# Operand rows at one position modulo 256 bytes, and short f16 products ahead of runs of weight products

## The chip, the core and the metric

The kernel runs on one core of a Trainium2 chip. The metric is the device time of one execution in microseconds; the median of several executions is compared.

## What is computed

The reference runs 256 tokens of width 1024 through two blocks, in float32. The first has two layers, each a mixer and a product-key expert layer (peer); the second has a feed-forward, a token mixer over 16 meta tokens and the 256 tokens, and another feed-forward.

```python
for layer in range(2):
    xn = rmsnorm(h, norm_mix[layer])
    h = h + (attn_retention_mixer if layer == 0 else short_conv_mixer)(xn, ...)
    h = h + peer(rmsnorm(h, norm_ffn[layer]), ...)
x = rmsnorm(h, final_norm)
...
h = h + 0.5 * swiglu(rms_norm(h, ffn1_norm), ffn1_w_in, ffn1_w_out)
h = h + token_mixer(rms_norm(h, mix_norm), ...)
h = h + 0.5 * swiglu(rms_norm(h, ffn2_norm), ffn2_w_in, ffn2_w_out)

def peer(xn, w_q, sub_keys, u, v):       # 8 heads x 2 key halves, 128 x 128 experts
    q = xn @ w_q                         # scores against the sub keys, top 16 of each half,
    gate = softmax(top 16 of the sums)   # top 16 of the 256 pairs
    return sum over chosen experts k of gate[k] * gelu(xn . u[k]) * v[k]
```

## The kernel before

**Tiling.** Activations lie transposed: 128 features on the partitions, tokens along the row, so that `h` is 8 chunks of 272 columns (16 meta tokens, then 256 tokens). Every expert is computed for every token in peer, and a gate matrix that is zero for those not chosen multiplies the result.

**Weight products.** Each weight tile is 128x1024 f32, 512 KB. `Weights` loads tiles on SP's queue three ahead (`wraw`), and splits each into a rounded part `whi` (ACT, line 177) and a rest `wlo` (DVE, line 178), three tiles ahead of their use. Activations are split in the same way (`split`, line 308). `mm3` (lines 303 to 306) makes one product of three: whi with the high part, whi with the low part, wlo with the high part, all fp32r. A weight tile is eight of these, 24 matmuls of 128x128 stationary weights against a moving row of 256 (or 272) columns. The moving rows are those of `xh`/`xl`, `ph`/`pl`, `ah`/`al`, `ch`/`cl`, `zh`/`zl`, `yh`/`yl` and `oh_`/`ol_`.

**Where the rows lie.** In the built program `xh` begins 128 bytes past a multiple of 256 in each partition and its rows are 272 x 4 = 1088 bytes, 64 past a multiple. Row c therefore begins at 128 + 64c, modulo 256; the slice without the meta columns (`XC`) begins 64 bytes later. A loop over c or j passes through the positions 0, 64, 128 and 192 in turn. The same holds for the 272-column `ph` and `ah` of the first feed-forward. The 256-column `ch`, `zh`, `ph`, `yh`, `oh_` and the `ah` of the last feed-forward have rows of 1024 bytes, and small pad tiles (`cpad`, `zpad`, `ppad`, `ypad`, `apad`) place all of their rows at 192. The moving `whi` of the first mixer (512 columns) and of the token mixer's value part (324) is not touched by the change.

**Stages.** In order: mixer0; for each layer peer's query stage (16 weight tiles, `ph` as moving operand), its u stage (128 tiles, `xh`, one c after another in a tile, two tiles for each PSUM tile `ps`), its v stage (128 tiles, `xh[:, j % 8, 0:256]`, 24 products on one row j, accumulated in four `acc` tiles); mixer1 between the layers; then ffn (272 columns), the token mixer, ffn (256 columns).

**What sets the order.** Code is written in the order in which it is to run. `bg` is a list of background tasks with costs; `bg.tick` after a weight tile issues some of them. In the u stages these are the scores (f32 products, line 780), top-16 searches on DVE, transposes, and from the middle on the gate products (`mult`, lines 940 and 941: 16 f16 products of 64 columns each time). In the v stages they go on up to j = 61. Other products come between weight tiles too: column sums (line 367), spreading of the norm (line 381), the flip products (1152, 1153), and the attention of the token mixer. So weight products come in runs that other products end.

```python
    def ft_tile(ps, n, cols=None, first=True):
        hi, lo = W.get()
        for c in range(8):
            s = slice(c * 128, c * 128 + 128)
            xh_, xl_ = n.x(c, cols)
            mm3(ps, hi[:, s], lo[:, s], xh_, xl_, first and c == 0, c == 7, skip_group_check=True)
```

Of the kernel before, what the change touches and what calls it, by code (L numbers as in the profile page):

```python
# [8 lines left out]
F32 = mybir.dt.float32  # L9
F32R = mybir.dt.float32r  # L10
# [11 lines left out]
META = 16  # L22
SEQ = 256
TALL = META + SEQ
HD2 = 64
GSCALE = 16384.0
TK_Q, TK_U, TK_G, TK_V = 1.2, 1.35, 72, 60
# [218 lines left out]


def _program(tc, nc, glob, wpool, mmp, accp, drp, ins, out, scat, stop):
    V, A, P = nc.vector, nc.scalar, nc.tensor

    h = glob.tile([128, 8, TALL], F32, name="h")
    xh = glob.tile([128, 8, TALL], F32R, name="xh")
    xl = glob.tile([128, 8, TALL], F32R, name="xl")
    ident = glob.tile([128, 128], F32, name="ident")
    ones = glob.tile([128, 2], F32, name="ones")
    gains = glob.tile([128, ins["gains"].shape[1]], F32, name="gains")

    glob.tile([128, 8], F32, name="gpad")
    W = Weights(nc, wpool, 3, 3)
    for nm in ("mix0_in", "mix0_out", "wq0", "u0", "v0", "mix1_in", "mix1_out", "wq1", "u1", "v1", "ffn1_in", "ffn1_out"):  # L260
        W.add(ins[nm])
# [14 lines left out]
            nc.scalar.dma_start(scat[l][:, i * n:i * n + n], src)  # L276
            cleared[l] += 1

    nc.scalar.dma_start(gains, ins["gains"])
    V.memset(ones, 1.0)  # L280
    A.activation(ones[:, 1:2], ones[:, 0:1], AF.Square)
    nc.gpsimd.dma_start(ident, ins["ident"])
# [18 lines left out]
        return accp.tile([128, 512], F32, tag="acc", name="acc")  # L301

    def mm3(ps, wh, wl, mh, ml, start, stop, **kw):
        P.matmul(ps, wh, mh, start=start, stop=False, **kw)  # L304
        P.matmul(ps, wh, ml, start=False, stop=False, **kw)  # L305
        P.matmul(ps, wl, mh, start=False, stop=stop, **kw)  # L306

    def split(hi, lo, src):
        A.copy(hi, src)  # L309
# [81 lines left out]
    class TwoNorms(Norm):  # L391


        def __init__(self, parts, sp, newps):
            super().__init__(("ffn1_norm_2", 0), 0, parts, newps)
            self.gf = col(("final_norm", 0))
            self.s1 = sp.tile([128, TALL], F32, name="s1")
            self.bc1 = sp.tile([128, TALL], F32, name="bc1")
            a, b = gcol[("final_norm", 0)], gcol[("ffn1_norm_2", 0)]
            self.gg = sp.tile([128, 8], F32, name="gg")  # L400
            self.m2 = sp.tile([128, 3], F32, name="m2")
            V.tensor_tensor(self.gg, gains[:, a:a + 8], gains[:, b:b + 8], op=ALU.mult)
            mg = sp.tile([128, 8, META], F32, name="mg")
            V.tensor_tensor(mg, h[:, :, 0:META], gains[:, b:b + 8, None].to_broadcast([128, 8, META]), op=ALU.mult)
            split(self.hi[:, :, 0:META], self.lo[:, :, 0:META], mg)
# [40 lines left out]
            for c in range(8):  # L446
                bg.add(0.45, lambda c=c: one(c))

    def ft_tile(ps, n, cols=None, first=True):

        hi, lo = W.get()
        for c in range(8):
            s = slice(c * 128, c * 128 + 128)
            xh_, xl_ = n.x(c, cols)
            mm3(ps, hi[:, s], lo[:, s], xh_, xl_, first and c == 0, c == 7, skip_group_check=True)
# [12 lines left out]
    def out_proj(nk, kh, kl, c0, scale, norm, last=None):  # L468

        T = TALL - c0  # L470
        for m in range(8):
            ps = mmtile()
            k = 0
            while k < nk:
                hi, lo = W.get()
                for kk in range(min(8, nk - k)):
                    s = slice(kk * 128, kk * 128 + 128)
                    mm3(ps[:, :T], hi[:, s], lo[:, s], kh(k), kl(k), k == 0, k == nk - 1)
                    k += 1
# [243 lines left out]
    def peer(l, n, close_parts, open_parts):  # L723
# [158 lines left out]
        def normed(c):  # L882
            t = glob.tile([128, TALL], F32, tag="nt", name="nxn", bufs=2)
            V.scalar_tensor_tensor(t[:, META:], h[:, c, META:], n.g(c), n.bc[:, META:], op0=ALU.mult, op1=ALU.mult)
            W.later(lambda: split(xh[:, c, META:], xl[:, c, META:], t[:, META:]))

        for q in range(16):
            if q % 2 == 0:
# [29 lines left out]
        def gates(half, newps, cost):  # L918
# [17 lines left out]
            def mult(q):  # L936
                a, bh, bl = st.pop(q)
                ps = newps()
                for t in range(8):
                    P.matmul(ps[:, t * 64:t * 64 + 64], a[:, t], bh[:, t], start=True, stop=False)  # L940
                    P.matmul(ps[:, t * 64:t * 64 + 64], a[:, t], bl[:, t], start=False, stop=True)
                st[("p", q)] = ps

            def fold(q):
# [51 lines left out]
        for jp in range(64):  # L996
# [59 lines left out]
    def ffn(c0, n, nxt, last=None, after=None):  # L1056
        T = TALL - c0
        cols = slice(c0, TALL)
        with tc.tile_pool(name=f"ffn{c0}", bufs=1) as sp:
            sp.tile([128, 48], F32, name="apad")  # L1060
            ah = sp.tile([128, 22, T], F32R, name="ah")
            al = sp.tile([128, 22, T], F32R, name="al")
            for i in range(22):
                pg, pu = mmtile(), mmtile()
                g0 = sp.tile([128, T], F32, name="fg0", bufs=2)
# [12 lines left out]
                        split(ah[:, i], al[:, i], u0)  # L1078
                    W.later(rest)

                ft_tile(pg[:, :T], n, cols)
                if i == 0:
                    n.sums()
                else:
# [5 lines left out]
                            after()  # L1090
                    gate()
                bg.tick(0.6)
                ft_tile(pu[:, :T], n, cols)
                if i == 0:
                    n.more()
                    first = gate, up
# [67 lines left out]
    def tokmix(n, BT, mknext):  # L1164
        with tc.tile_pool(name="tok", bufs=1) as sp:
# [235 lines left out]
            def kq_tiles(b):  # L1401
                t0, t1 = BATCH[b]
                for i in range(t0, t1):
                    ps = mmtile()
                    ft_tile(ps[:, (0 if is_key(i) else META):TALL], n, slice(0 if is_key(i) else META, TALL))
# [39 lines left out]

            for i in range(16):
                ps = mmtile()
                ft_tile(ps[:, :256], n, XC)
                tick()
                if i > 11 and busy():  # L1450
                    a_step()
# [14 lines left out]
            for m in range(8):  # L1466
                pf, pw = mmtile(), mmtile()
                hi, lo = W.get()
                if m < 7:
                    sigm(m + 1)  # L1470
                for k in range(8):
# [12 lines left out]

    pools = []

    def open_parts(make, T=SEQ):
# [4 lines left out]
        hi = sp.tile([128, 8, T], F32R, name="ph")  # L1492
        lo = sp.tile([128, 8, T], F32R, name="pl")
        sp.tile([128, 72], F32, name="ppad")
        return make((hi, lo), sp)

# [80 lines left out]
```

## Time and profile before

| | |
|---|---|
| median of 3 runs | 2455.16 us (2449.33 to 2455.28) |
| the profiled execution | 2454.97 us |
| its span, first to last instruction | 2453.2 us |
| TensorE matmul busy | 2427.3 us, 99%, 20410 records |
| VectorE busy | 1841.1 us, 75% |
| ScalarE busy | 1208.5 us, 49% |
| GpSimd busy | 643.0 us, 26% |
| mean rate of the DMAs | 189 GB/s |

Matmuls are pipelined: each record lasts longer than the distance to the next start, so their durations add up to more than the span. The distance between starts is read from a timeline, or as a stretch divided by the records in it. A window counts every record that touches it, so two products or so that began before its edge are in its count.

### The profile page before, as it was taken

To read this page: it belongs to the slowest core of one execution; us is meant where nothing else is said; L and a number is where in the kernel's file an instruction comes from. 1 tells how busy PE (TensorE), PEld (TensorE's weight loads), DVE (VectorE), ACT (ScalarE), POOL (GpSimd) and SP (SyncE) were. 2 spreads that over 40 slices of the span, in tenths; PEclk is the share of its full clock that TensorE was granted. 3 is DMA by queue.
4 is the path that set the end of the run, shared out by engine and by line. 5 is a ranking of instruction groups with operands and counts; after the bars stand their busy time and mean duration, and the time that the engine had idled before them with its cause. 6 is when DMAs were issued, how large, how long until landed. Compare 5 with 4: busy or idle time off the path is not lost.

```text
span 2453.2 us, 50327 instructions
## 1 busy us (share of the span) xinstructions
PE 2427.3 (99%) x20410; PEld 2363.4 (96%) x20410; DVE 1841.1 (75%) x3514; ACT 1208.5 (49%) x1745; POOL 643.0 (26%) x421
## 2 busy tenths in 40 slices
PE   8999999999999999999999999999999999999999
PEld 6799999999999999999999999999999999779999
DVE  6688896877986667788977869976677655667764
ACT  4555555444444445555554444444455443446543
POOL 0007787802320000037877403310010000100000
PEclk9999999999999999999999999999999999999999
DMA  7578887765666665667777656666655555325555
GB/s 241 171 247 218 224 225 191 173 189 192 196 206 204 215 204 186 196 177 174 180 184 178 181 175 204 202 203 212 210 191 182 173 174 172 114 95 174 188 185 168
DMA packets 170650, 464.37 MB, mean 189 GB/s; under 512 B 52369, under 2 KB 54425, under 8 KB 169905
## 3 DMA queue, kind: packets, MB, share of 16 engines
q1 hardware_dynamic: 117440, 420.04, 53.1%
q0 software_dynamic: 43616, 24.27, 7.7%
q10 hardware_dynamic: 9360, 16.84, 1.8%
q8 instruction: 160, 2.62, 0.4%
q14 instruction: 74, 0.60, 0.1%
HBM read 443.09 MB, written 17.99 MB: 188 GB/s over the span
## 4 chain that ended last, share of the span: by engine, by line
PE 91%; DVE 6%; ACT 1%; DMA 1%; issue 0%; SPq 0%; ACTq 0%; DVEq 0%
PE mm L304 18%; PE mm L306 18%; PE mm L305 18%; PE acc L304 10%; PE acc L305 10%; PE acc L306 10%; DVE wlo L178 2%; PE mm L639 1%; PE mm L640 1%; PE mm L638 1%; PE acc L1205 1%; PE acc L780 1%; ACT whi L177 0%; DVE Hb L790 0%; DVE Hb L788 0%
## 5 line engine op out<-in xcount | busy, mean ns | idle before, releaser
L178 DVE TENSOR_TENSOR wlo<-wraw,whi 128x1024 fp32r<-128x1024 f32 (+2 forms) x799 | 996.3, 1250 | 444.1 <-ACT whi L177 437.2
L177 ACT CAST whi<-wraw 128x1024 fp32r<-128x1024 f32 (+2 forms) x799 | 833.2, 1044 | 664.1 <-PE mm L305 217.1
L304 PE MATMUL mm<-xh,whi 128*128 128x256 f32 (+1 forms) x2632 | 744.0, 283 | 0.0
L306 PE MATMUL mm<-xh,wlo 128*128 128x256 f32 (+1 forms) x2632 | 741.3, 282 | 0.5
L305 PE MATMUL mm<-xl,whi 128*128 128x256 f32 (+1 forms) x2632 | 741.2, 282 | 0.0
L304 PE MATMUL acc<-xh,whi 128*128 128x256 f32 x2048 | 577.5, 282 | 0.3
L305 PE MATMUL acc<-xl,whi 128*128 128x256 f32 x2048 | 574.5, 281 | 0.2
L306 PE MATMUL acc<-xh,wlo 128*128 128x256 f32 x2048 | 574.4, 280 | 0.0
L852 POOL DMA_INDIRECT gates<-gt,idx x256 | 482.1, 1883 | 220.3 <-DVE idx L842 94.8
L304 PEld LDWEIGHTS mm<-xh,whi 128*128 128x128 f32 x2632 | 497.8, 189 | 7.8 <-issue 7.3
L306 PEld LDWEIGHTS mm<-xh,wlo 128*128 128x128 f32 x2632 | 498.3, 189 | 1.7 <-DVE wlo L178 1.7
L305 PEld LDWEIGHTS mm<-xl,whi 128*128 128x128 f32 x2632 | 495.0, 188 | 0.0
L304 PEld LDWEIGHTS acc<-xh,whi 128*128 128x128 f32 x2048 | 387.4, 189 | 0.7 <-ACT xh L309 0.7
L305 PEld LDWEIGHTS acc<-xl,whi 128*128 128x128 f32 x2048 | 386.2, 189 | 0.5 <-DVE xl L310 0.5
L306 PEld LDWEIGHTS acc<-xh,wlo 128*128 128x128 f32 x2048 | 386.5, 189 | 0.0
L306 PE MATMUL mm<-ph,wlo 128*128 128x256 f32 (+1 forms) x800 | 228.3, 285 | 5.6 <-DVE wlo L178 5.6
L304 PE MATMUL mm<-ph,whi 128*128 128x256 f32 (+1 forms) x800 | 228.9, 286 | 0.0
L305 PE MATMUL mm<-pl,whi 128*128 128x256 f32 (+1 forms) x800 | 227.3, 284 | 0.0
L306 PEld LDWEIGHTS mm<-ph,wlo 128*128 128x128 f32 x800 | 152.1, 190 | 6.4 <-DVE wlo L178 6.4
L1011 ACT ACTIVATE Hb<-mm 128x512 f32<-128x512 f32 x112 | 67.2, 600 | 180.4 <-PE mm L306 174.8
L305 PEld LDWEIGHTS mm<-pl,whi 128*128 128x128 f32 x800 | 151.4, 189 | 0.3
L304 PEld LDWEIGHTS mm<-ph,whi 128*128 128x128 f32 x800 | 151.2, 189 | 0.1
(359 smaller groups left out, 3052.9 us busy)
## 6 DMA issues: line engine op xcount, KB each, us to landing
wraw<-in_u SPq DMA_DIRECT2D x256, 512.0 KB
wraw<-in_v SPq DMA_DIRECT2D x256, 512.0 KB
wraw<-in_ffn_in SPq DMA_DIRECT2D x88, 512.0 KB
wraw<-in_mix_in SPq DMA_DIRECT2D x52, 512.0 KB
gates<-zt ACTq DMA_DIRECT2D x64, 256.0 KB
wraw<-in_wq SPq DMA_DIRECT2D x32, 512.0 KB
gj<-gates POOLq DMA_DIRECT2D x64, 256.0 KB
wraw<-in_ffn_out SPq DMA_DIRECT2D x32, 512.0 KB
```

The lines of the kernel that those rows point to most:

```text
L177: self.nc.scalar.copy(hi[:, :cols], raw[:, :cols])
L178: self.nc.vector.tensor_tensor(lo[:, :cols], raw[:, :cols], hi[:, :cols].bitcast(F32), op=ALU.subtract)
L304: P.matmul(ps, wh, mh, start=start, stop=False, **kw)
L305: P.matmul(ps, wh, ml, start=False, stop=False, **kw)
L306: P.matmul(ps, wl, mh, start=False, stop=stop, **kw)
L638: P.matmul(ps[tt], xa, hi[:, w], start=(c == 0), stop=False)
L639: P.matmul(ps[tt], xa, lo[:, w], start=False, stop=False)
L640: P.matmul(ps[tt], xb, hi[:, w], start=False, stop=(c == 7))
L780: P.matmul(t[:, i * 128:i * 128 + 128], qT[:, q, tt * 128:tt * 128 + 128], sk[:, q], start=True, stop=True)
L852: b = nc.gpsimd.indirect_dma_start(out=flat, out_offset=bass.IndirectOffsetOnAxis(ap=idx[:, i:i + 1], axis=0), in_=gt0[:, i:i + 1], in_off ...
L1011: A.activation(Haf[:, j * 256:j * 256 + 512] if j < NA else Hbf[:, (j - NA) * 256:(j - NA) * 256 + 512], ps, AF.Gelu)
L1205: P.matmul(t[:, s], KQ[pr, qt, q], KQ[pr, kt, 0:k], start=True, stop=True)
```

## The change

Rows of `xh` and `xl` become 320 floats (1280 bytes, five times 256) and a pad of 64 bytes ahead of them places every row at 192; the 256 token columns that the u stage reads stand in the last 256 floats of a row, which is 192 too. The 272-column `ph` and `ah` get rows of 320 floats of which the last 272 are used, from 192 on. `ones` moves into the tile `gains`, and `gpad` goes.

`P` becomes a wrapper that notes when a product other than a weight product or a gate product has been issued (`broken`). `settle`, called before the first product of a run's first weight tile, then issues four f16 products of 64 columns of `ident` with itself into the PSUM tile that the run is about to overwrite. It isn't called for the second tile of a `ps` in the u stage, for the single tiles of the token mixer, nor in a feed-forward while background tasks are waiting. `mult` of the gates counts as such a lead itself.

```diff
+ROW = 320
...
+    class Other:
+        broken = True
+        def matmul(self, *a, **k):
+            self.broken = True
+            return T_.matmul(*a, **k)
...
+    P = Other()
...
-    xh = glob.tile([128, 8, TALL], F32R, name="xh")
-    xl = glob.tile([128, 8, TALL], F32R, name="xl")
+    glob.tile([128, 16], F32, name="xpad")
+    xh = glob.tile([128, 8, ROW], F32R, name="xh")
+    xl = glob.tile([128, 8, ROW], F32R, name="xl")
...
+    def settle(ps):
+        if P.broken:
+            k = ident.bitcast(F16)
+            for _ in range(4):
+                T_.matmul(ps[:, 0:64], k[:, 0:128], k[:, 0:64], start=True, stop=True)
+            P.broken = False
...
-    def ft_tile(ps, n, cols=None, first=True):
+    def ft_tile(ps, n, cols=None, first=True, steady=True):
         hi, lo = W.get()
+        if first and steady:
+            settle(ps)
...
                 hi, lo = W.get()
+                if k == 0:
+                    settle(ps)
...
-                ft_tile(ps[:, s * 256:s * 256 + 256], xn, XC, s == 0)
+                ft_tile(ps[:, s * 256:s * 256 + 256], xn, slice(ROW - SEQ, ROW), s == 0)
...
-            ah = sp.tile([128, 22, T], F32R, name="ah")
+            ah = sp.tile([128, 22, row], F32R, name="ah")[:, :, row - T:]
...
-                ft_tile(pg[:, :T], n, cols)
+                ft_tile(pg[:, :T], n, cols, steady=not bg.q)
...
-    n = peer(1, made["n"], close_parts, lambda: open_parts(lambda pr, sp: TwoNorms(pr, sp, mmtile), TALL))
+    n = peer(1, made["n"], close_parts, lambda: open_parts(lambda pr, sp: TwoNorms(pr, sp, mmtile), ROW))
```

On TensorE the first u stage, behind scores that follow the second tile of a PSUM tile. Before (line 780 is the scores; 304 to 306 the weight products):

```order
L305 MATMUL mm<-xl,whi 128x256
L306 MATMUL mm<-xh,wlo 128x256
L780 MATMUL acc<-Hb 128x128 x4
L304 MATMUL mm<-xh,whi 128x256
L305 MATMUL mm<-xl,whi 128x256
```

After (line 258 is the wrapper, 329 the new products, 320 to 322 the weight products):

```order
L321 MATMUL mm<-xl,whi 128x256
L322 MATMUL mm<-xh,wlo 128x256
L258 MATMUL acc<-Hb 128x128 x4
L329 LDWEIGHTS ident
L329 MATMUL mm<-ident 128x64
L329 LDWEIGHTS ident
L329 MATMUL mm<-ident 128x64
L329 LDWEIGHTS ident
L329 MATMUL mm<-ident 128x64
L329 LDWEIGHTS ident
L329 MATMUL mm<-ident 128x64
L320 MATMUL mm<-xh,whi 128x256
```

Four f16 products stand between the scores and the weight products. There are 28 such places and 112 new products in the program.

Also on TensorE in the first u stage, behind scores that fall between the two tiles of a PSUM tile. Before:

```order
L306 MATMUL mm<-xh,wlo 128x256
L780 MATMUL acc<-Hb 128x128 x4
L304 MATMUL mm<-xh,whi 128x256
L305 MATMUL mm<-xl,whi 128x256
L306 MATMUL mm<-xh,wlo 128x256
```

After:

```order
L322 MATMUL mm<-xh,wlo 128x256
L258 MATMUL acc<-Hb 128x128 x4
L320 MATMUL mm<-xh,whi 128x256
L321 MATMUL mm<-xl,whi 128x256
L322 MATMUL mm<-xh,wlo 128x256
```

Nothing moved here; the four new products come 24 weight products later, ahead of the next PSUM tile. On DVE, ACT, POOL and SP no instruction is added, removed or moved.

## Rows read from the trace of the kernel before

**Rows 1.** The page, busy time and the chain that ended last.

```profile
PE 2427.3 (99%) x20410; PEld 2363.4 (96%) x20410; DVE 1841.1 (75%) x3514; ACT 1208.5 (49%) x1745; POOL 643.0 (26%) x421
...
PE 91%; DVE 6%; ACT 1%; DMA 1%; issue 0%; SPq 0%; ACTq 0%; DVEq 0%
```

**Rows 2.** Groups by form: count, busy us, mean ns of one, idle before.

```profile
L304 PE MATMUL mm<-xh,whi 128*128 128x256 f32 x2592 | 732.0, 282 | 0.0
...
L304 PE MATMUL acc<-xh,whi 128*128 128x256 f32 x2048 | 577.5, 282 | 0.3
...
L306 PE MATMUL mm<-ph,wlo 128*128 128x256 f32 x448 | 126.4, 282 | 5.6 <-DVE wlo L178 5.6
...
L304 PE MATMUL mm<-ph,whi 128*128 128x272 f32 x352 | 102.0, 290 | 0.0
...
L304 PE MATMUL mm<-ah,whi 128*128 128x272 f32 x176 | 50.7, 288 | 0.0
...
L304 PE MATMUL mm<-ah,whi 128*128 128x256 f32 x176 | 48.6, 276 | 0.0
...
L304 PE MATMUL mm<-zh,whi 128*128 128x256 f32 x64 | 18.0, 281 | 0.0
...
L304 PE MATMUL mm<-yh,whi 128*128 128x256 f32 x64 | 17.7, 276 | 0.0
```

**Rows 3.** Stretches of weight products: window us, length, busy (count), clock, DMA.

```profile
744.00:904.00 160.00, 160.00 (x1353) 1.00 0.66 211
948.00:1009.00 61.00, 61.00 (x520) 1.00 0.57 186
2393.00:2449.00 56.00, 56.00 (x496) 1.00 0.59 179
2274.00:2388.00 114.00, 114.00 (x966) 1.00 0.56 185
1900.00:1976.00 76.00, 76.00 (x605) 1.00 0.52 170
1978.00:2040.00 62.00, 62.00 (x499) 1.00 0.60 179
```

**Rows 4.** Windows on four xh rows in turn, v stage: 192, 0, 64, 128.

```profile
620.88:623.49 2.61, 2.61 (x25) 1.00 0.59 220
623.49:626.35 2.86, 2.86 (x27) 1.00 0.48 115
626.35:629.18 2.83, 2.83 (x27) 1.00 0.88 317
629.18:632.03 2.85, 2.85 (x27) 1.00 0.65 216
```

**Rows 5.** TensorE's timeline, gate products to weight products: start us, duration us, line.

```profile
620.20 0.20 PE L940 MATMUL mm<-gbh,ga 128*128 128x64 f16 x1
...
620.68 0.36 PE L304 MATMUL acc<-xh,whi 128*128 128x256 f32 x1
620.88 0.28 PE L305 MATMUL acc<-xl,whi 128*128 128x256 f32 x1
620.99 0.28 PE L306 MATMUL acc<-xh,wlo 128*128 128x256 f32 x1
```

**Rows 6.** TensorE's timeline in mixer1, four f32 products to weight products.

```profile
947.55 0.64 PE L381 MATMUL mm<-ident,nry 128*128 128x128 f32 x4
947.95 0.36 PE L304 MATMUL mm<-ph,whi 128*128 128x256 f32 x1
948.15 0.28 PE L305 MATMUL mm<-pl,whi 128*128 128x256 f32 x1
948.27 0.28 PE L306 MATMUL mm<-ph,wlo 128*128 128x256 f32 x1
```

**Rows 7.** Windows, all engines: length, PE, PEld, DVE, ACT, POOL busy (count).

```profile
190.00:370.00 180.00, 179.77 (x1518) 179.16 (x1517) 161.74 (x469) 101.97 (x118) 140.02 (x74) 1.00 0.84 220
570.00:735.00 165.00, 164.97 (x1585) 164.29 (x1586) 149.13 (x214) 78.90 (x112) 56.18 (x46) 1.00 0.62 199
```

**Rows 8.** Whom TensorE waited for: us in total, times, longest.

```profile
PE mm L306 <- DVE wlo L178: 5.6, 4, 2.4
```

More of the change, by code (lines that the diff above doesn't have):

```diff
@@ L248, in _program, with transpose @@
 def _program(tc, nc, glob, wpool, mmp, accp, drp, ins, out, scat, stop):
-    V, A, P = nc.vector, nc.scalar, nc.tensor
+    V, A, T_ = nc.vector, nc.scalar, nc.tensor
+    class Other:
[3 more added lines that the diff above has]
+            return T_.matmul(*a, **k)
+        def transpose(self, *a, **k):
+            self.broken = True
+            return T_.transpose(*a, **k)
+    P = Other()
     h = glob.tile([128, 8, TALL], F32, name="h")
-    xh = glob.tile([128, 8, TALL], F32R, name="xh")
-    xl = glob.tile([128, 8, TALL], F32R, name="xl")
+    glob.tile([128, 16], F32, name="xpad")
+    xh = glob.tile([128, 8, ROW], F32R, name="xh")
+    xl = glob.tile([128, 8, ROW], F32R, name="xl")
     ident = glob.tile([128, 128], F32, name="ident")
-    ones = glob.tile([128, 2], F32, name="ones")
-    gains = glob.tile([128, ins["gains"].shape[1]], F32, name="gains")
-    glob.tile([128, 8], F32, name="gpad")
+    ng = ins["gains"].shape[1]
+    gains = glob.tile([128, ng + 2], F32, name="gains")
+    ones = gains[:, ng:ng + 2]
     W = Weights(nc, wpool, 3, 3)
@@ L277, in zero @@
             cleared[l] += 1
-    nc.scalar.dma_start(gains, ins["gains"])
+    nc.scalar.dma_start(gains[:, 0:ng], ins["gains"])
     V.memset(ones, 1.0)
@@ L303, in mm3 @@
     def mm3(ps, wh, wl, mh, ml, start, stop, **kw):
-        P.matmul(ps, wh, mh, start=start, stop=False, **kw)
-        P.matmul(ps, wh, ml, start=False, stop=False, **kw)
-        P.matmul(ps, wl, mh, start=False, stop=stop, **kw)
+        T_.matmul(ps, wh, mh, start=start, stop=False, **kw)
+        T_.matmul(ps, wh, ml, start=False, stop=False, **kw)
+        T_.matmul(ps, wl, mh, start=False, stop=stop, **kw)
+    def settle(ps):
[4 more added lines that the diff above has]
+            P.broken = False
     def split(hi, lo, src):
@@ L404, in __init__ @@
             V.tensor_tensor(mg, h[:, :, 0:META], gains[:, b:b + 8, None].to_broadcast([128, 8, META]), op=ALU.mult)
-            split(self.hi[:, :, 0:META], self.lo[:, :, 0:META], mg)
+            o = self.hi.shape[2] - TALL
+            split(self.hi[:, :, o:o + META], self.lo[:, :, o:o + META], mg)
             V.tensor_tensor(mg, h[:, :, 0:META], h[:, :, 0:META], op=ALU.mult)
@@ L884, in normed @@
             V.scalar_tensor_tensor(t[:, META:], h[:, c, META:], n.g(c), n.bc[:, META:], op0=ALU.mult, op1=ALU.mult)
-            W.later(lambda: split(xh[:, c, META:], xl[:, c, META:], t[:, META:]))
+            W.later(lambda: split(xh[:, c, ROW - SEQ:], xl[:, c, ROW - SEQ:], t[:, META:]))
         for q in range(16):
@@ L939, in mult @@
                 for t in range(8):
-                    P.matmul(ps[:, t * 64:t * 64 + 64], a[:, t], bh[:, t], start=True, stop=False)
-                    P.matmul(ps[:, t * 64:t * 64 + 64], a[:, t], bl[:, t], start=False, stop=True)
+                    T_.matmul(ps[:, t * 64:t * 64 + 64], a[:, t], bh[:, t], start=True, stop=False)
+                    T_.matmul(ps[:, t * 64:t * 64 + 64], a[:, t], bl[:, t], start=False, stop=True)
+                P.broken = False
                 st[("p", q)] = ps
@@ L1059, in ffn @@
         with tc.tile_pool(name=f"ffn{c0}", bufs=1) as sp:
-            sp.tile([128, 48], F32, name="apad")
-            ah = sp.tile([128, 22, T], F32R, name="ah")
-            al = sp.tile([128, 22, T], F32R, name="al")
+            row = ROW if T == TALL else T
+            if row == T:
+                sp.tile([128, 48], F32, name="apad")
+            ah = sp.tile([128, 22, row], F32R, name="ah")[:, :, row - T:]
+            al = sp.tile([128, 22, row], F32R, name="al")[:, :, row - T:]
             for i in range(22):
@@ L1092, in ffn @@
                 bg.tick(0.6)
-                ft_tile(pu[:, :T], n, cols)
+                ft_tile(pu[:, :T], n, cols, steady=not bg.q)
                 if i == 0:
@@ L1404, in kq_tiles @@
                     ps = mmtile()
-                    ft_tile(ps[:, (0 if is_key(i) else META):TALL], n, slice(0 if is_key(i) else META, TALL))
+                    ft_tile(ps[:, (0 if is_key(i) else META):TALL], n, slice(0 if is_key(i) else META, TALL), steady=False)
                     held.append((i, ps))
@@ L1447, in tokmix @@
                 ps = mmtile()
-                ft_tile(ps[:, :256], n, XC)
+                ft_tile(ps[:, :256], n, XC, steady=False)
                 tick()
@@ L1468, in tokmix @@
                 hi, lo = W.get()
+                settle(pw)
                 if m < 7:
@@ L1485, in _program, with open_parts @@
     pools = []
-    def open_parts(make, T=SEQ):
+    def open_parts(make, row=SEQ):
         p = tc.tile_pool(name=f"parts{len(pools)}", bufs=1, side="right")
@@ L1491, in open_parts @@
         pools.append(p)
-        hi = sp.tile([128, 8, T], F32R, name="ph")
-        lo = sp.tile([128, 8, T], F32R, name="pl")
+        hi = sp.tile([128, 8, row], F32R, name="ph")
+        lo = sp.tile([128, 8, row], F32R, name="pl")
         sp.tile([128, 72], F32, name="ppad")
```

## The prediction

> **What bounds the kernel now.** I read the page's busy shares first, then the groups of matmuls by form, then stretches of pure weight products, then the starts at a few seams. TensorE is busy 99% of the span and carries 91% of the chain that ended last [rows 1]. The reader is to see that nothing else has to be late for the end to move: the time is the number of products times the distance from one start to the next. That distance is not the 276 to 290 ns of the groups, since products overlap, but their means already hint at the point: same shape, same line, 282 ns on xh, 281 on zh, 276 on yh and on ah [rows 2].
>
> The distance itself is a stretch divided by its count (less two, for products begun before the edge) [rows 3]: 160/1351 = 118.4 ns in the v stage, 114/964 = 118.3 in the last ffn's first half, where xh rows rotate through the four positions 0, 64, 128 and 192 past a multiple of 256; 61/518 = 117.8 on ph, whose rows all lie at 192; 56/494 = 113.4 on the last ah, all at 192 too. With 272 columns, 76/603 = 126.0 and 62/497 = 124.7.
>
> Two things therefore set it. **Position:** in the v stage one xh row serves 24 products, and four such rows in turn took 2.61, 2.86, 2.83 and 2.85 us [rows 4]. Divided by the 23 or 24 starts each window holds, that is 113.5 ns for the row at 192 and 119.2, 117.9, 118.8 for those at 0, 64 and 128. **Entry:** position is not enough. The row at 192 was entered from 16 short f16 gate products, and its second and third products already start 0.11 us apart [rows 5]; the ph stretch, equally at 192, was entered from four f32 products and its products start 0.12 apart at once [rows 6] and for the next 61 us [rows 3]. So a run has a fast and a slow pitch at the same address, and keeps the one that it entered with. Why, no row shows.
>
> **The change part by part.** *Pads.* No engine gets an instruction more for them; of DVE, ACT, POOL and SP only names of tiles change. All 256-column weight products on xh now start at 192, as do the 272-column ones on ph and ah; the few 272-column ones on xh in the token mixer go to 128 and stay as they are. *Lead.* 28 calls of settle add 112 f16 products of 64 columns. What they change is the entry.
>
> The gain, from 256 columns, against 113.4:
> - xh rotating per row triple (line 304 to 306 on mm): 2592 x 3 = 7776 products [rows 2]. The token mixer's 576 are single tiles behind f32 products, not led, at 118 now and later: no gain. Another 96 (four second halves in the u stages that follow scores, as the order shows) stay slow. 7104 x (118.3 - 113.4) = 34.8 us.
> - xh in the v stage: 2048 x 3 = 6144 [rows 2]. The 3600 behind the last gate (two runs of 1800) at 118.4: 18.0. In the 2544 before that, one row in four is at 113.5 already, mean 117.3: 2544 x 3.9 = 9.9. Together 27.9 us.
> - ph, 448 x 3 = 1344 [rows 2], of which 144 are not led. At most 1200 x 4.4 = 5.3; but 282 ns is a mean over runs at both pitches, so I take 3.5 and keep 2.5 to 5.3.
> - ch and zh: 384 x 4.4 = 1.7 us. oh_, yh and the last ah go at 113.4 already: nothing.
>
> Sum 67.9 us. **272 columns:** (352 + 176) x 3 = 1584 products at a mean of 125.5. No stretch before has them all at 192. If they get the fast pitch, it is 113.4 plus 16 columns at 106.7/256 ns each = 120.1, so 8.5 us; if that size has no fast pitch, 0. Runs behind the flip products are not led either. I take 4.
>
> **The cost of the lead.** The 16 gate products begin at 620.20 and the weight product after them at 620.68: 30 ns each [rows 5], so four cost 0.12 us and 28 leads 3.4. The first weight product takes 0.20 us to the second behind f16 [rows 5] and behind f32 products [rows 6], so nothing is saved or lost there. An f32 product followed by an f16 one is in no row; the nearest price is that 0.20, the dearest start, so 0 to 5.6 more. I take 4 in all, 3.4 to 9.0.
>
> **What is late next.** A tile of 24 products shrinks from about 2.84 to 2.72 us while DVE's work per tile stays. DVE is busy 161.7 of 180 us in the first half of u and 149.1 of 165 in the first half of v [rows 7], twice each; after the change 161.7 of 172.7 and 149.1 of 159.8, both 93 to 94%. It fits, but in lumps (the top-16 searches) that a lookahead of three tiles must even out. PE waits for wlo now 5.6 us in four waits [rows 8]. I add 4 us, 0 to 10.
>
> Net: 67.9 + 4 - 4 - 4 = 64 us. The profiled execution took 2454.97 us (span 2453.2), within 0.2 of the median 2455.16, so no correction: 2455 - 64 = **2391**.
>
> **A rule against it.** The rows say that the distance at 256 columns is 113.4 or 117.8 at one address and up to 119.2 at others. The Trainium skill ("TensorE: Matmul & The Clock Gate", section Back-to-back issue gap) gives a warm gap of N/2.4 + 2.5 ns, with no term for where the operand lies or what came before; for 256 columns that makes 109.2 ns, an estimate by that page. By it the pads are worth nothing; the trace agrees with neither the figure nor the absence of a position.
>
> **The rivals.**
> - *DVE becomes the bound* in the first halves of u and v. For: 90% there already, top-16 work in lumps. Against: only 5.6 us of waits now. If nothing is won there: 2 x 1488 x 4.9 = 14.6 and 2 x 1344 x 3.9 = 10.5 lost, 25 instead of the 4 allowed: 2412.
> - *The short products of ident do not give the fast entry.* For: only gate products are seen to do it, 16 of them, not 4. Against: same kind, same columns. Then the runs behind settle, 5016 on xh, 216 from ch, 1344 from ph and 408 from oh_ (counted in the order) go at 117.8: 6984 x 4.4 = 30.7 more, and the 4 of the 272s lost: 2426.
> - *The position is worth nothing by itself* (the page's rule as a mechanism of this kernel: the pattern of rows 4 belongs to something else that turns with j). Then only the leads' 4 us are left: 2459, no measurable change. Against: 113.4 on ah and yh, which are other tiles in other stages.
> - *Slower: slow entry everywhere.* The rotation of positions is what lets a run find the fast pitch; with all rows at 192 every run holds the slow one. Then rotating products gain 0.5 x 13,300 = 6.6, the 912 of oh_, yh and ah lose 4.0, the 636 fast rows of v lose 2.8, and dear leads cost 9.0: 9.2 slower, 2464. It is slower beyond measure as soon as a lead costs over 0.26 us. For: the 61 us of ph at one position and slow. Against: rows 5, fast from the second start.
>
> **How the numbers follow.** Forecast 2391, chance 0.79; DVE bound 2412, 0.09; lead without effect 2426, 0.06; nothing 2459, 0.04; slower 2464, 0.02. About 0.3% (7 us) is what a measurement can tell from no change. Faster 0.94, same 0.04, slower 0.02. The forecast's own ends: ph +1.8, 272 columns +4.5, leads +0.6, DVE +4 give 2380; the other ends -1, -4, -5, -6 give 2407. Reaching to the DVE case, the range is 2379 to 2413.
>
> **What would show it.** Right: xh groups at about 276 ns mean; a long v stretch with 113.4 ns from start to start; the four-row pattern gone; ph behind an f16 lead at 0.11 from its second start; 28 leads of some 0.12 us; PE's waits for wlo under 15 us. Wrong: xh at 281 (entry or position fails, and whether gate-led and settle-led runs differ says which); PE idle before line 322 of tens of us (DVE); ph and ah at 272 columns still 287 to 290 would take only the 4 us.

## The result, and the profile after

The changed kernel takes 2397.47 us (median of four runs, 2396.45 to 2400.15), the kernel before 2453.86 beside it: ratio 0.9775, interval 0.9758 to 0.9792. The prediction was 2391, range 2379 to 2413. The profiled execution took 2397.68 us, its span is 2395.9, so 57.3 us of span are gone where 64 were forecast.

The page, busy time and the chain that ended last, of the kernel after:

```profile
PE 2368.1 (99%) x20522; PEld 2306.1 (96%) x20522; DVE 1839.9 (77%) x3514; ACT 1210.2 (51%) x1745; POOL 651.2 (27%) x421
...
PE 91%; DVE 5%; DMA 1%; ACT 1%; issue 1%; SPq 0%; ACTq 0%; DVEq 0%
```

Against [rows 1] TensorE has 112 records more (28 leads of four) and 59 us less to do; nothing else moved into the chain. TensorE's groups by form (count, busy us, mean ns of one, idle before), as in [rows 2]; the three lines of `mm3` are now L320 to L322:

```profile
L320 PE MATMUL mm<-xh,whi 128*128 128x256 f32 x2592 | 726.4, 280 | 0.0
...
L320 PE MATMUL acc<-xh,whi 128*128 128x256 f32 x2048 | 568.4, 278 | 0.5 <-ACT xh L333 0.5
...
L320 PE MATMUL mm<-ch,whi 128*128 128x256 f32 x64 | 18.1, 282 | 0.0
...
L320 PE MATMUL mm<-yh,whi 128*128 128x256 f32 x64 | 18.0, 281 | 0.0
...
L320 PE MATMUL mm<-zh,whi 128*128 128x256 f32 x64 | 17.7, 276 | 0.0
```

`xh` came to 280 and 278, between the 276 and the 281 that the prediction had named as signs of right and wrong. `zh` fell from 281 to 276, `ch` did not, and `yh`, which was at 276, rose to 281. How far apart the products start is seen in windows (window, length and busy us with the records in it, then clock and DMA share):

```profile
744.00:904.00 160.00, 160.00 (x1414) 1.00 0.68 217
...
192.00:214.00 22.00, 22.00 (x189) 1.00 0.87 239
245.00:266.00 21.00, 21.00 (x188) 1.00 0.86 235
```

```profile
220.00:229.50 9.50, 9.50 (x83) 1.00 0.74 219
232.00:241.00 9.00, 9.00 (x82) 1.00 1.00 261
1888.00:1960.00 72.00, 72.00 (x586) 1.00 0.57 175
2190.00:2210.00 20.00, 20.00 (x172) 1.00 0.63 194
```

Counted as in the prediction (two less than the records): the v stage went from 118.4 to 160/1412 = 113.3 ns. Two stretches of the first u stage, both on `xh` at 192, both led by four short products, run at 22/187 = 117.6 and 21/186 = 112.9 (the edges make about 0.5 of that; the starts below say 113.4). The 272-column `ph` runs at 72/584 = 123.3, `yh` at 20/170 = 117.6. The pair from 220 and from 232 is one run, slow (9.5/81 = 117.3) and then fast (9/80 = 112.5); between them a new tile's first product on `wlo` starts 0.30 us behind its neighbour, where 0.12 is usual (timeline: start us, duration us):

```profile
230.40 0.28 PE L321 MATMUL mm<-xl,whi 128*128 128x256 f32 x1
230.70 0.38 PE L322 MATMUL mm<-xh,wlo 128*128 128x256 f32 x1
230.93 0.28 PE L320 MATMUL mm<-xh,whi 128*128 128x256 f32 x1
```

What stood ahead of the two u stretches, on the same timeline; first the slow one:

```profile
189.36 0.28 PE L322 MATMUL mm<-ph,wlo 128*128 128x256 f32 x1
189.48 0.29 PE L329 MATMUL mm<-ident 128*128 128x64 f16 x4
189.61 0.36 PE L320 MATMUL mm<-xh,whi 128*128 128x256 f32 x1
189.81 0.28 PE L321 MATMUL mm<-xl,whi 128*128 128x256 f32 x1
...
190.87 0.28 PE L321 MATMUL mm<-xl,whi 128*128 128x256 f32 x1
```

and the fast one:

```profile
241.81 0.72 PE L258 MATMUL acc<-Hb 128*128 128x128 f32 x5
242.37 0.28 PE L329 MATMUL mm<-ident 128*128 128x64 f16 x4
242.49 0.37 PE L320 MATMUL mm<-xh,whi 128*128 128x256 f32 x1
242.69 0.28 PE L321 MATMUL mm<-xl,whi 128*128 128x256 f32 x1
...
243.72 0.28 PE L321 MATMUL mm<-xl,whi 128*128 128x256 f32 x1
```

Both leads take 0.12 to 0.13 us and both first products 0.20. Then nine distances take 1.06 us in the one, 117.8 ns each, and 1.03 in the other, 114.4. The slow one has weight products ahead of its lead: the f32 products fell on a PSUM tile's second half, where `settle` isn't called, and 24 unled weight products lie between. Of the 16 led runs on `xh` in the two u stages 10 enter slow, and so do the two led runs on `ph` that follow scores in the query stages: 12 of 18, and all 12 have weight products ahead of their lead. All 64 runs behind the sixteen gate products enter fast.

Where the 57 us are, by summing the distances between neighbouring starts of both traces (those over 150 ns, which hold a first product or a wait, apart as gaps):

| part | predicted | measured |
|---|---|---|
| `xh` rotating: u stages; last feed-forward and token mixer | 34.8 | 23.0 + 5.8 = 28.8 |
| `xh` in the v stages | 27.9 | 27.9 |
| `ph`, 256 columns | 3.5 | 3.8 |
| `ch` and `zh` | 1.7 | 0 + 1.1 |
| `oh_`, `yh` | 0 | -0.7 - 0.9 |
| 272 columns, `ph` and `ah` | 4 (0 to 8.5) | 3.0 + 0.8 |
| 112 short products | -4 | -3.4 |
| more gaps in runs of weight products | -4 (0 to -10) | -5.1 |
| start of the kernel, f32 and other products | 0 | +2.0 |
| sum | 64 | 57.3 |

Two of these rows don't say what they seem to. **The gaps.** Inside its runs TensorE did not wait more than before. Distances over 150 ns inside a run are 27 in both traces, 13.5 us before and 13.2 after. What grew is first products: 14 of the leads stand between weight products and so make a first product, 0.20 us ahead of the second, where there was an ordinary distance. That is 2.8 of the 5.1 us, for 1.7 less in the rows of the steady distances. **The clock.** The granted clock stood at 0.50 (1.2 of 2.4 GHz) in four stretches of the execution profiled before, 17 us in all, and in two of the one after, 6.8 us, while TensorE was busy. Here is one of each, both in `ph` products:

```profile
172.60:176.00 3.40, 3.40 (x19) 0.50 1.01 249
```

```profile
1041.40:1044.80 3.40, 3.40 (x18) 0.50 0.81 274
```

Both programs issue the same 20410 products in the same order, the leads apart, so that distances can be compared one by one. Those in the half-clock stretches of either trace differ by 4.3 us, which the change didn't bring. Without them some 53 of the 57.3 us are left, and `ph` with 256 columns gives 2.0 instead of 3.8.

### The profile page after: what moved, and what is told of

Its sections match the earlier page's. It is cut to its first block, busy times and chain, and to the rows that moved or that the text cites. A ratio compares the mean times of both kernels' runs of the same rounds, so it can differ in the third digit from the quotient of the medians.

```text
span 2395.9 us, 50539 instructions
## 1 busy us (share of the span) xinstructions
PE 2368.1 (99%) x20522; PEld 2306.1 (96%) x20522; DVE 1839.9 (77%) x3514; ACT 1210.2 (51%) x1745; POOL 651.2 (27%) x421
## 4 chain that ended last, share of the span: by engine, by line
PE 91%; DVE 5%; DMA 1%; ACT 1%; issue 1%; SPq 0%; ACTq 0%; DVEq 0%
PE mm L320 19%; PE mm L322 18%; PE mm L321 18%; PE acc L320 10%; PE acc L321 9%; PE acc L322 9%; PE acc L258 3%; PE mm L258 2%; DVE wlo L179 2%; PE acc L262 1%; ACT whi L178 1%; DMA wraw<-in_mix_in 1%; DMA wraw<-in_u 0%; DMA wraw<-in_wq 0%; PE acc L969 0%
## 5 line engine op out<-in xcount | busy, mean ns | idle before, releaser
L320 PE MATMUL mm<-xh,whi 128*128 128x256 f32 (+1 forms) x2632 | 738.4, 281 | 0.0
L322 PE MATMUL mm<-xh,wlo 128*128 128x256 f32 (+1 forms) x2632 | 731.4, 278 | 1.1 <-DVE wlo L179 1.0
L321 PE MATMUL mm<-xl,whi 128*128 128x256 f32 (+1 forms) x2632 | 730.8, 278 | 0.0
L320 PE MATMUL acc<-xh,whi 128*128 128x256 f32 x2048 | 568.4, 278 | 0.5 <-ACT xh L333 0.5
L321 PE MATMUL acc<-xl,whi 128*128 128x256 f32 x2048 | 565.7, 276 | 0.2
L322 PE MATMUL acc<-xh,wlo 128*128 128x256 f32 x2048 | 565.4, 276 | 0.0
L881 POOL DMA_INDIRECT gates<-gt,idx x256 | 489.1, 1910 | 216.7 <-DVE idx L871 101.1
L320 PEld LDWEIGHTS mm<-xh,whi 128*128 128x128 f32 x2632 | 494.3, 188 | 7.4 <-issue 6.9
L322 PEld LDWEIGHTS mm<-xh,wlo 128*128 128x128 f32 x2632 | 494.2, 188 | 2.5 <-DVE wlo L179 2.3
L320 PEld LDWEIGHTS acc<-xh,whi 128*128 128x128 f32 x2048 | 384.5, 188 | 0.9 <-ACT xh L333 0.9
L322 PEld LDWEIGHTS acc<-xh,wlo 128*128 128x128 f32 x2048 | 384.4, 188 | 0.0
L322 PE MATMUL mm<-ph,wlo 128*128 128x256 f32 (+1 forms) x800 | 227.1, 284 | 4.5 <-DVE wlo L179 4.5
L320 PE MATMUL mm<-ph,whi 128*128 128x256 f32 (+1 forms) x800 | 228.0, 285 | 0.0
L322 PEld LDWEIGHTS mm<-ph,wlo 128*128 128x128 f32 x800 | 152.1, 190 | 4.9 <-DVE wlo L179 4.9
L320 PEld LDWEIGHTS mm<-ph,whi 128*128 128x128 f32 x800 | 152.0, 190 | 0.1
```

The source lines that it names most:

```text
L320: T_.matmul(ps, wh, mh, start=start, stop=False, **kw)
L321: T_.matmul(ps, wh, ml, start=False, stop=False, **kw)
L322: T_.matmul(ps, wl, mh, start=False, stop=stop, **kw)
L881: b = nc.gpsimd.indirect_dma_start(out=flat, out_offset=bass.IndirectOffsetOnAxis(ap=idx[:, i:i + 1], axis=0), in_=gt0[:, i:i + 1], in_off ...
```

## The experiments

Two theories of the lead at first. **Chance**: what the four short products give is chance, and they buy about what they cost. **Place**: they do bring runs into the fast pitch, but only where they stand directly behind what interrupted. (The letters in the expectations are each expectation's own.)

**Pads without leads.**

```diff
     def settle(ps):
-        if P.broken:
+        if False:
```

> The changed kernel with no lead: the rows keep their new positions, the 28 groups of four short f16 products are gone. Theory A (the position carries nearly all; a run behind f32 products finds either pitch by chance, so the leads buy about what they cost, 3.4 us, and what runs behind oh_ and yh lost, 1.6 us, comes back): the v stages unchanged at 113.4 ns per product, the whole 2394 to 2404 us. Rival B (the lead is needed: every run behind f32 products is slow without it): the 3768 products in runs that the leads made fast lose 4.5 ns each, 17 us, less 3.4 for the leads: about 2411 us.

2395.17 us, ratio 0.9785 (0.9768 to 0.9801). Its windows for the v stage, for the stretch of u that was fast, and for `oh_` and `yh`:

```profile
744.00:904.00 160.00, 160.00 (x1414) 1.00 0.66 217
...
245.00:266.00 21.00, 21.00 (x180) 1.00 0.81 223
```

```profile
2180.00:2200.00 20.00, 20.00 (x173) 1.00 0.59 187
```

The u stretch is at 21/178 = 118.0 here, yet over both u stages the distances fell by 22.9 us, as with leads: other runs are fast, for no reason that the trace shows. `oh_` and `yh` are slow (20/171 = 117.0) without a lead too. The v stages are as fast as with leads (160/1412 = 113.3), and the time lies in the first theory's 2394 to 2404, not at the rival's 2411. The gain comes from the pads; what the four short products add can't be told from nothing.

**Leads without pads.**

```diff
-ROW = 320
+ROW = 272
```

with the 64 bytes of pad behind `xl` instead of ahead of `xh`, so that rows take up their old positions again.

> The kernel before with the leads alone: xh rows of 1088 bytes from 128 past a multiple of 256 as before, 272-column rows of ph and ah as before, 28 leads. Theory A (a lead acts only where all rows stand at 192): ph and zh win about 4 us, the leads cost 3.4, oh_ and yh lose 1.6 if their entry turns slow: 2452 to 2457 us, no change. Rival B (the entry is what was slow, wherever the rows lie): runs on xh at 113.4 ns, about 2400 us.

2452.13 us, ratio 1.0014 (1.0004 to 1.0024): no gain, as the first theory had it (2452 to 2457), and not the rival's 2400. The v stage holds 1353 records in its 160 us, as many as before:

```profile
744.00:904.00 160.00, 160.00 (x1353) 1.00 0.64 210
```

**A lead at the second half as well**, in the query and u stages, so that it always stands directly behind the interrupting products:

```diff
         if first and steady:
             settle(ps)
+        elif both and P.broken:
+            settle(ps)
+            first = True
```

> The changed kernel with the lead directly behind the products that interrupt, also at the second tile of a PSUM tile in the u and query stages (there the first weight product starts its own columns afresh). As many leads, but none of them behind weight products any more in the first halves of u. Theory A (four short products give the fast pitch directly behind f32 products, and the slow one directly behind weight products): the u stages fall from 114.8 to about 113.5 ns between steady starts, 6072 x 1.3 = 8 us: about 2389 us. Rival B (four products are too few and the pitch behind them is chance): as many slow runs as in the changed kernel, 2394 to 2401 us.

2392.57 us, ratio 0.9777 (0.976 to 0.9793). All 14 led runs of the u stages enter fast (no run goes without a lead now), the distances there fall by 30.4 us (the prediction had 29 to 30 for them), `oh_` and `yh` are fast again, `ch` is not. The stretch that was slow:

```profile
192.00:214.00 22.00, 22.00 (x197) 1.00 0.91 247
```

22/195 = 112.8. So the theory of place holds for these runs; elsewhere `ch` and two runs of 24 behind column sums, led in the same way, are slow. But the time, between the 2389 of the one theory and the 2394 of the other, can't be told from that with pads alone: the gaps in u and v grew by 6.0 us over before, against 3.4 in the changed kernel, and here they lie inside runs (39 such in the whole program, 19.4 us, against 27 and 13.2).

**How many short products?** The changed kernel with n of them, n = 0 to 13 in turn, ahead of each of the last 56 rows of both v stages, written into a spare PSUM tile; in the second layer one f32 product of 128 columns stands ahead of them.

```diff
+            if j >= 64:
+                t = mmtile()
+                k = ident.bitcast(F16)
+                if l == 1:
+                    T_.matmul(t[:, 0:128], ident, ident, start=True, stop=True)
+                for _ in range((j - 64) % 14):
+                    T_.matmul(t[:, 0:64], k[:, 0:128], k[:, 0:64], start=True, stop=True)
```

> The changed kernel with a lead ahead of each row j from 64 to 119 of both v stages (all rows at 192): (j - 64) mod 14 short products of ident into a spare PSUM tile, so each count from 0 to 13 four times in each layer; in the second layer one f32 product of ident stands ahead of them. Read is the pitch of the 24 weight products behind each lead. Theory A (what stands ahead of the lead decides): in the first layer 4 gives the slow pitch, as behind weight products in the changed kernel, and some larger count the fast one, as the 16 gate products do; in the second layer any count from 1 on gives the fast pitch. Rival B (the count alone decides): the same counts are fast in both layers. Rival C (ident as operand is at fault, not the count): all counts slow in the first layer. The leads add some 112 x (6.5 x 30 + 90) ns = 32 us and the f32 products about 10.

The run took 2447.99 us, 50 more than the changed kernel where some 42 were expected; what is read is the pitch. Every count gave the same in all four of its occurrences. Three neighbours on the timeline, each row's first product and the lead of the next:

```profile
751.44 0.26 PE L1072 MATMUL mm<-ident 128*128 128x64 f16 x3
751.54 0.36 PE L320 MATMUL acc<-xh,whi 128*128 128x256 f32 x1
...
754.37 0.29 PE L1072 MATMUL mm<-ident 128*128 128x64 f16 x4
754.49 0.36 PE L320 MATMUL acc<-xh,whi 128*128 128x256 f32 x1
...
757.41 0.32 PE L1072 MATMUL mm<-ident 128*128 128x64 f16 x5
757.56 0.37 PE L320 MATMUL acc<-xh,whi 128*128 128x256 f32 x1
...
760.39 0.35 PE L1072 MATMUL mm<-ident 128*128 128x64 f16 x6
```

From first product to next lead, 24 products: 2.83 us behind three, 2.92 behind four, 2.83 behind five. Behind weight products four and twelve give 118 ns, and 1 to 3, 5 to 11 and 13 all give 113; eight is fast from its second start. Behind the f32 product 0, 1, 4 and 12 are slow, the others fast. So C is out; A was right of the first layer and wrong of the second, where not every count from 1 on is fast; B holds for every count but 1. The change's four is one of the two bad counts. The gates' sixteen, on which the prediction leaned, lies outside the sweep.

**Two instead of four.**

```diff
-            for _ in range(4):
+            for _ in range(2):
```

> The changed kernel with two short products in each lead instead of four; nothing else differs. Count theory (the number of short products modulo 8 decides, and four is the one bad count): every led run goes at 113.4 ns from its first products, those led directly behind weight products (slow in the changed kernel: first u stage at 156, 189, 218, 270, 300, 353 us) too. Against the changed kernel: u stages 7 us less in steady distances, ch 0.8, oh_ and yh 1.5, leads 1.7 less (56 fewer at 0.030), of which up to 4 may come back as waits for the low halves of weights: 2386 to 2391 us, ratio to before 0.973 to 0.975. Rival, what stands ahead of the lead decides, not the count: the same runs stay slow, 2396 us, ratio 0.977. Rival, two are too few: nearly all led runs slow, 2412 us, ratio 0.983.

2391.3 us, ratio 0.9755 (0.9741 to 0.9768). All 16 led runs of u and the two of the query stages enter fast, the twelve among them. The same place as the slow lead above:

```profile
188.88 0.28 PE L322 MATMUL mm<-ph,wlo 128*128 128x256 f32 x1
189.00 0.23 PE L329 MATMUL mm<-ident 128*128 128x64 f16 x2
189.07 0.37 PE L320 MATMUL mm<-xh,whi 128*128 128x256 f32 x1
189.27 0.28 PE L321 MATMUL mm<-xl,whi 128*128 128x256 f32 x1
...
190.30 0.28 PE L321 MATMUL mm<-xl,whi 128*128 128x256 f32 x1
```

The same nine distances take 1.03 us, as behind the good lead. Not every led run does: behind column sums or the spreading of the norm three short ones are slow (24, 72 and 48 products, from 919.55, 1011.79 and 2208.15 us), so two is good behind weight products and not everywhere. Against the changed kernel the distances in u fall by 7.3 us, `ch`, `oh_` and `yh` by 2.5, the short products by 1.6: 11.4. The span fell by 6.4 only, since the gaps in u grew by 4.6. Whom TensorE waited for (us in total, times, longest), after and with two:

```profile
PE mm L322 <- DVE wlo L179: 5.5, 4, 2.4
PE mm L258 <- DVE wlo L179: 2.4, 4, 1.0
```

```profile
PE mm L322 <- DVE wlo L179: 9.3, 13, 2.2
PE mm L258 <- DVE wlo L179: 1.4, 3, 0.6
```

The waits for the low halves of weights went from 7.9 to 10.7 us, in 16 instead of 8 places; in the u stages alone from 1.0 to 3.8, which is 2.8 of the 4.6. Behind three such waits runs of u fell from the fast pitch to the slow one (292.7, 1095.7 and 1150.7 us). The expectation's upper end was 2391; it had allowed up to 4 for returning waits. The pitches, more than the time, rule out the rivals (2396 and 2412).

**Two, at both halves.** The edit of the run with both halves, and two for four.

> Two short products, and in the query and u stages also ahead of the second half of a PSUM tile where that one follows the interrupting products. Count theory: pitches as with two at the first half, and the four blocks of 24 products that run unled get 113.4 as well, 96 x 4.5 = 0.4 us less; no difference that can be measured from the run with two: 2386 to 2391, ratio 0.973 to 0.975. Rival, place decides (lead directly behind the interrupting products is what helps): this one is 5 to 10 us below the run with two at first halves alone.

2390.77 us, ratio 0.975 (0.9737 to 0.9763): the same as with two alone, so the rival (5 to 10 us below it) is out: where the lead stands makes no difference that can be measured once the count is a good one. One of the 14 led runs of u enters slow all the same (216.25 us), behind the same eight score products as others that enter fast. This is the lowest median of the study, 2.5% below the kernel before; neither it nor the run with two alone, which is the simpler edit, can be told from the changed kernel by these intervals.

**Twelve instead of four** (the same line, 12).

> Twelve short products in each lead, four plus one period of eight. Count theory: the same runs are slow as with four, behind weight products 118 ns, oh_ and yh 117.8, ch 117.8; time that of the changed kernel plus 28 x 8 x 0.030 = 6.7: 2404 us. Rival, more short products settle better (sixteen gate products always do): all runs at 113.4, 7104 on xh and oh_, yh, ch; 9 us less, 2395 us.

2400.83 us in one run, span 2399.0, 3.1 above the changed kernel's. The same twelve runs of u enter slow; the stretch from 192:

```profile
192.00:214.00 22.00, 22.00 (x189) 1.00 0.88 233
```

the 189 records of the changed kernel. The rival (2395, all fast) is out for u. A miss in the other direction: `oh_` and `yh` are fast behind twelve and slow behind four, and the gaps in u are 2.4 us smaller, so the time is 3 us below the 2404 expected. Eight more short products are not in every place the same lead.

**Eight positions in turn.** Two short products and rows of 1248 bytes, 32 less than five times 256:

```diff
-ROW = 320
+ROW = 312
```

> Two short products, and rows padded to 1248 instead of 1280 bytes, so that eight rows in turn lie at 160, 128, 96, 64, 32, 0, 224, 192 past a multiple of 256; the weights stay at multiples of 256. In a v stage 24 products in turn use one row, so the stage gives a pitch for each position in one state of entry. Position theory: 192 at 113.4, 0, 64 and 128 at 119.2, 117.9, 118.8 as in the kernel before, also behind this good lead; which of 32, 96, 160 and 224 are fast is not known: if none is, 13,920 products lose 7/8 of 4.9, 60 us, 2449 us; if the four odd ones are, about 3/8 of 4.9, 26 us, 2414 us. Rival, the count of the lead does everything and position nothing: all eight at 113.4 and 2388 us. The 272-column rows of the token mixer pass the eight positions too: if 192 is only poor for that length, some other position shows about 120.

2447.76 us in one run: nearly all the gain is gone, and the time is near the position theory's 2449. One round through the rows in the v stage, 24 products each, took 2.83 us at 64, 2.80 at 32, 2.88 at 0, 2.85 at 224, 2.83 at 192, then 2.85, 2.85 and 2.88 at 160, 128 and 96. The rows at 64 and at 192:

```profile
745.33:748.16 2.83, 2.83 (x26) 1.00 0.60 195
...
756.69:759.52 2.83, 2.83 (x27) 1.00 0.57 188
```

These windows run from start to start, so 24 distances each: 117.9, 116.7, 120.0, 118.8, 117.9, 118.8, 118.8, 120.0. No position is fast, not even 192, which took 2.61 us for such a row in [rows 4]. There the run had just come from the gate products; here it began at 728 us, 28 us and ten rows earlier, with gate products ahead of the row at 0. But turning alone doesn't take the pitch away. Two more rows at 192 of this kernel, one row behind gate products that stood ahead of the row at 224, and two rows behind those ahead of the row at 0:

```profile
590.02:592.77 2.75, 2.75 (x26) 1.00 0.18 40
733.92:736.75 2.83, 2.83 (x26) 1.00 0.58 187
```

and one of the kernel before, two rows behind gate products ahead of the row at 64:

```profile
596.55:599.27 2.72, 2.72 (x26) 1.00 0.88 247
```

That is 114.6, 117.9 and 113.3 ns. So a run can carry the fast pitch through rows elsewhere, and what a row at 192 gets depends on how its run was entered: on which row, how long ago, or both, which these runs don't part. Both theories missed 192 in a long run of turning rows. The 272-column rows took 125.2 ns on average in this kernel; taken row by row, 123.4 to 126.2, so none of the eight positions was near 120.

**One position kept, another than 192.** That leaves two readings: any position will do if it is kept, or only 192. Two short products, and all of `xh` and `xl` at 64, at 0 and at 128 by another pad ahead (and one behind, so that the weights stay at multiples of 256); the 272-column `ah` goes with them. At 64:

```diff
-    glob.tile([128, 16], F32, name="xpad")
+    glob.tile([128, 48], F32, name="xpad")
     ...
     xl = glob.tile([128, 8, ROW], F32R, name="xl")
+    glob.tile([128, 32], F32, name="xpad2")
```

> Two short products in each lead, and all 256-column rows of xh and xl at 64 past a multiple of 256 instead of 192; the 272-column rows of ah also at 64. Everything else keeps its place (the weights stay at multiples of 256). Theory 192 is special: 13,920 products on xh at 117.9 as in the kernel before, 13,920 x 4.5 = 63 us more than the run with two: 2454 us. Rival, what matters is that one position is kept (a run holds the fast pitch as long as its rows don't move against 256, which the eight positions in turn, 117.8 at 192 too, suggest): 113.4 on xh, 2391 us. ah with 272 columns: 123.3 at 192; at 120 if 192 is only poor for that length.

> The same with xh, xl and the 272-column ah at 0 past a multiple of 256, where the stationary weights start as well. Theory 192 is special: 119.5 on xh, 13,920 x 6.1 = 85 us more: 2476 us. Rival, one kept position is enough: 113.4, 2391 us. In between, a pitch that depends on the position but is the same at every product: some value between, read from the v stage.

> The same with xh, xl and the 272-column ah at 128. Theory 192 is special: 118.7 on xh, 13,920 x 5.3 = 74 us more: 2465 us. Rival, one kept position is enough: 113.4, 2391 us.

2445.27, 2470.2 and 2456.58 us in one run each, against 2454, 2476 and 2465 expected of "192 is special" and 2391 of "one kept position". The same 160 us of the v stage, at 64, at 0 and at 128:

```profile
744.00:904.00 160.00, 160.00 (x1361) 1.00 0.64 212
```

```profile
744.00:904.00 160.00, 160.00 (x1335) 1.00 0.63 209
```

```profile
744.00:904.00 160.00, 160.00 (x1351) 1.00 0.64 210
```

117.7, 120.0 and 118.6 ns, with the same good lead: within 1 ns the prices that the four rows in turn had shown. The rival is out. The times lie 6 to 9 us below the expectations, mostly since slower products leave 5.5, 9.3 and 7.1 us less of gaps in u and v than the run with two. The last feed-forward shows the entry again: its `ah` stayed at 192 in all three, in one run with the `xh` products ahead of it, and goes at 117.8 behind `xh` at 64 and at 113.4 behind `xh` at 0 or 128. At 272 columns `ah` took 126.7, 125.3 and 126.7 against 123.3 at 192: that length likes 192 best too, and no position that was tried brings it to 120. Only the moving rows were moved: whether their own place counts, or their place against the weight tiles, which stay at multiples of 256, no run parts, and the counts of the lead were swept at 192 alone.

## Why the prediction was right, and where it was not

**Position** was right, and is shown: moving the rows back costs all the gain (leads without pads), and of the four places tried only 192 runs at 113.4. The v term, 27.9 us, came out to the decimal, since the runs that start there all start behind sixteen gate products. (The two runs behind the last gates have 1776 products each, not 1800, which moves the term by 0.2 us at most.)

The rule of the Trainium skill ("TensorE: Matmul & The Clock Gate", section Back-to-back issue gap) that spoke against it makes 109.2 ns of 256 columns, an estimate by that page, wherever the operand lies. That section of the Trainium skill calls the rule the gap of an isolated product, which the prediction left out; for a stream of products with their weight loads it has measured figures, about 81 ns at 128 columns and 131 at 512, and none at 256. No run here shows 109.2; kept positions gave 113.4, 117.7, 118.6 and 120.0, and the measurement decides. The rival built on it, 2459, did not happen.

**Entry** was right as far as it went: a run keeps the pitch it came in with, 117.6 and 113.4 on the same rows. The step that failed is "same kind, same columns", by which four short products of `ident` were taken for sixteen of the gates. Four is a bad count behind weight products: 10 of 16 led runs in u came in slow. That is the mechanism of the second rival (2426), in part. It is why rotating `xh` gave 28.8 and not 34.8 us, `ch` nothing, and `oh_` and `yh`, which were fast before without a lead, 1.6 us of loss where the prediction had "nothing". With two in place of four the u stages give 30.3 and the three small runs are fast. "Keeps the one that it entered with" is too strong as well: a wait within a run can change it, to the fast pitch (220 and 232 us above) or to the slow one (with two short products).

**Cost of the lead**: the short products took 3.4 us in 28 leads, the 30 ns a piece read from [rows 5]. "Nothing is saved or lost there" holds behind other products only: the 14 leads between weight products add a first product each, 0.20 us in place of 0.12, 1.2 us in all. The dearest end, 0.20 us more each, did not show: 0.12 us from lead to first product behind f32 products as behind weight products.

**272 columns**: 3.8 us, by luck near the middle taken. The pitch at 192 is 123.3, neither 120.1 nor 125.5.

**What is late next**: DVE did not become the bound; the page has it at 77%. In the same stretch as [rows 7] it is busy 162.72 us of 180 and TensorE still 179.41:

```profile
190.00:370.00 180.00, 179.41 (x1557) 178.49 (x1556) 162.72 (x471) 104.10 (x121) 141.82 (x74) 1.00 0.84 223
```

The row of the gaps has 5.1 us where 4 were taken, but by luck: the 4 were for waits on DVE, and those in the u stages came to 1.0 us; most of the 5.1 is first products and a half-clock stretch. Waits come back with the next gain: with two short products 4.6 of another 11.4 us are more gaps in u, 2.8 of them waits for DVE's low halves. In lumps, DVE is the next limit of the u stages.

So 64 became 57 by three things: 6.0 on rotating `xh`, 2.2 on `ch`, `zh`, `oh_` and `yh` (1.7 expected, 0.5 lost), 1.1 more in gaps; 2.7 came back from cheaper leads, `ph`, and the f32 and other products. The clock's 4.3 us are luck as well: without them the forecast was 11 us too high rather than 7.

## What to carry over

Where TensorE is busy to the end, read the distance from one start to the next, not the mean duration: 4% of it, and 2.2% of the kernel's time, lay in the place of the moving operand modulo 256 bytes, and pads alone bought that. When a trick is inferred from one pattern seen in the trace (sixteen short products), copy that pattern or sweep its size; the number that you pick instead may be the one that does nothing. Before a difference between two traces is shared out among causes, compare their granted clocks. Before the bottleneck is made faster, see how little slack its feeder has: two fifths of the last gain went into gaps.

## What the runs showed of the hardware

- 256-column products of rounded f32 by 128x128 weights start 113.4 ns apart with their rows kept at 192 past a multiple of 256 bytes, 117.7 at 64, 118.6 at 128, 120.0 at 0. Where rows turn, a row at 192 takes 113.3 to 114.7 or 117.8 to 118.0, by how its run was entered.
- At 192 there are two pitches, 113.4 and 117.8. Which one a run gets depends on the number of short f16 products ahead of it: 4 and 12 slow, 1 to 3, 5 to 11 and 13 fast behind weight products. What stands ahead of them matters as well: one f32 product of 128 columns makes 1 slow too, and behind the f32 products of the u stage four are fast. A wait within a run can change the pitch either way.
- With 272 columns the best was 123.3 ns, at 192; others took 125 to 127.
- Where the granted clock was 0.50, 256-column products started 213 to 214 ns apart, on `ph` kept at 192 (before, 172.6 to 176.0) and on `xh` rows that turn (leads without pads, 2136.0 to 2139.4) alike: the place of the rows showed only at full clock.

Why 192, why four and twelve, and why a run without a lead is fast in one kernel and slow in the next, the traces don't show. That stays open.
